# First expert's rows by one-hot products and a hand-written tail: two layers of hybrid attention with a mixture of experts

## The chip, the cores and the metric

One NeuronCore of one Trainium2 chip runs the whole program. The metric is the time of one execution on the device in microseconds (us), the median of several runs. Engines are named as the profile names them: PE (TensorE, with PEld for its weight loads), DVE (VectorE), ACT (ScalarE), POOL (GpSimd) and SP (SyncE, which issues most transfers). L626 is line 626 of the kernel.

## What is computed

Two layers over 512 tokens of 1,024 columns in f32. Each layer mixes tokens by 16 attention heads, adds the result to the residual, normalises, and sends each token to 2 of 16 experts.

```
for l in range(2):
    mix = hybrid_mixer(x, ...)          # 8 MLA heads and 8 sparse (DSA) heads of 64 columns, then @ w_o
    x = layer_norm(ALPHA * x + mix, ln1_g[l], ln1_b[l])
    ffn = grouped_moe(x, ...)           # router, then top-2 of 16 experts
    x = layer_norm(ALPHA * x + ffn, ln2_g[l], ln2_b[l])

# grouped_moe
aff = sigmoid(xt @ router_w); biased = aff + router_bias
g_sel = argmax over 4 groups of (sum of the 2 best biased of the group's 4)
e_idx = the 2 best experts of that group; wts = aff[e_idx] / sum
act = silu(xt @ w_gate[e]) * (xt @ w_up[e]) * gate
out = sum over e of act @ w_down[e]     # 1024 -> 512 -> 1024
```

## The kernel before

**Precision.** A weight is split on the chip into a high and a low f32r part (a *granule*: 128 x 1024 values; `granule`, L163 casts on ACT, L164 subtracts on DVE or POOL), and a product is made of three matmuls (high x high, low x high, high x low). Transposes and the value products of attention run in plain f32; each such product leaves two records in the trace.

**Attention.** `softmax_T` makes one head's probabilities: scores on PE, minimum on DVE, Exp on ACT, scaling on DVE, then four groups of transposes on PE (L499) which ACT copies to SBUF (L501, `pt[kb]`). `pv` multiplies the values of two heads with these copies (L508): per head four products of 512, 384, 256 and 128 columns. The two heads of a pair have 64 output columns each and write the two halves, partitions 0 to 63 and 64 to 127, of one or of two PSUM tiles. The order of the heads is the string `HEADS` (`m0 m1d0 m2d1 m3d2 d3`); which instruction comes next on an engine is set by the framework's scheduler from priorities (`tc.issue_after` shifts one, a manual dependency adds a wait), unless it stands in a `manual_schedule`.

**From the last projection to the first expert.** `mix` multiplies the mixed heads with `w_o` (L626, 384 matmuls a layer) for four tiles of 128 tokens; tile t + 1 runs two steps (`LAG`) behind tile t. `half` then does, for one half of a tile's columns, the residual (L635, DVE), its statistics (L636), four transposes (L190), ACT's copy and the router's logits (L645, PE). `norm` finishes the tile: mean and variance, rsqrt on POOL (L185), the centred and scaled `x1` (L661, L667; for the last tile ACT L669 and POOL L670), the logits `lg` (L663, L664), and the transfer of `x1` to HBM (`xdr`). `route` selects experts with some twenty small DVE operations (L769 to L798) and gives each token a place in its expert's list of at most CAP rows (L805, L809). `warm` issues products that nobody reads (L200).

**Experts.** `fetch(e)` makes one-hot columns of an expert's list (L893), turns them into row numbers with four small matmuls (`index`, L909, L910), and POOL issues an indirect transfer of the 128 rows (L899). `rows_T` transposes the rows (L190) and splits them into `xh`, `xl`; `gate_up` (L931, L932) and `down` (L953) follow, expert by expert, with the next experts' steps placed between products by the table `between`. Before the first expert the largest count is read into registers (L1041), and all engines branch (L1044) over a body for lists longer than CAP, `overflow`; with these inputs the body doesn't run.

Weights come by SP's queue into a pool of 12 tiles of 128 x 2048 (`bigt`), some three experts ahead. PSUM has the pools "mm" (4 tiles), "tr" (2) and "pv" (2).

## Time and profile before

| | |
|---|---|
| median of 3 runs | 1271.31 us (1266.88 to 1273.93) |
| the profiled execution | 1272.13 us, span 1270.3 us |
| busy: PE / DVE / ACT / POOL | 1196.8 / 1040.6 / 805.5 / 313.5 us |
| mean granted clock of PE | 0.968 |
| layer 0: first attention products to the last projection | 140 to 238.4 us |
| layer 0: end of the last projection to the first expert product | 283.25 to 316.04 us |
| layer 0: experts at full pace | 319 to 550 us |

The span runs from the first to the last instruction. Busy times are sums over the span, so an engine with a low share can still be the one that others wait for within a stage; the stages have to be read apart.

### The profile page before, as it was taken

To read this page: it belongs to the slowest core of one execution; us is meant where nothing else is said; L and a number is where in the kernel's file an instruction comes from. 1 tells how busy PE (TensorE), PEld (TensorE's weight loads), DVE (VectorE), ACT (ScalarE), POOL (GpSimd) and SP (SyncE) were. 2 spreads that over 40 slices of the span, in tenths; PEclk is the share of its full clock that TensorE was granted. 3 is DMA by queue.
4 is the path that set the end of the run, shared out by engine and by line. 5 is a ranking of instruction groups with operands and counts; after the bars stand their busy time and mean duration, and the time that the engine had idled before them with its cause. 6 is when DMAs were issued, how large, how long until landed. Compare 5 with 4: busy or idle time off the path is not lost. (4 is left out here: it accounts for less than half of the span.)

```text
span 1270.3 us, 17037 instructions
## 1 busy us (share of the span) xinstructions
PE 1196.8 (94%) x5821; PEld 926.8 (73%) x5821; DVE 1040.6 (82%) x1855; ACT 805.5 (63%) x1262; POOL 313.5 (25%) x241
## 2 busy tenths in 40 slices
PE   9999999996999999999898999999969999999995
PEld 6777555785888888887687775557858888888873
DVE  4689956387999999998858899563779999999897
ACT  4523567532888888887535245665328888888883
POOL 2334323113111111110542343322231111112005
PEclk9989999998999999999898899999989999999998
DMA  7616103374899999987335160033758999999941
GB/s 269 192 45 195 53 1 132 133 265 146 326 390 372 384 385 381 377 323 298 99 128 161 34 231 2 32 115 125 260 192 319 385 385 394 381 376 373 328 169 67
DMA packets 57264, 292.91 MB, mean 231 GB/s; under 512 B 10194, under 2 KB 14034, under 8 KB 28752
## 3 DMA queue, kind: packets, MB, share of 16 engines
q1 hardware_dynamic: 47376, 270.48, 58.3%
q0 software_dynamic: 8352, 16.00, 3.5%
q10 hardware_dynamic: 1440, 5.24, 1.0%
q8 instruction: 49, 0.80, 0.2%
q14 instruction: 47, 0.39, 0.1%
HBM read 269.01 MB, written 31.98 MB: 237 GB/s over the span
## 5 line engine op out<-in xcount | busy, mean ns | idle before, releaser
L163 ACT CAST hl<-big 128x1024 fp32r<-128x1024 f32 x446 | 465.0, 1054 | 147.5 <-PE mm L932 56.5
L164 DVE TENSOR_TENSOR hl<-big,hl 128x1024 fp32r<-128x1024 f32 x407 | 490.0, 1230 | 58.5 <-ACT hl L163 51.3
L931 PE MATMUL mm<-hl,xh 128*128 128x512 f32 x512 | 211.4, 413 | 0.9 <-ACT xh L163 0.9
L932 PE MATMUL mm<-hl,xh 128*128 128x512 f32 x512 | 201.2, 393 | 0.0
L953 PE MATMUL pv<-hl,hT 128*128 128x512 f32 x720 | 169.8, 390 | 2.9 <-DVE big L963 2.9
L953 PEld LDWEIGHTS pv<-hl,hT 128*128 128x128 f32 x720 | 134.8, 188 | 31.8 <-DVE big L963 3.6
L271 PE MATMUL mm<-big,hl 128*128 128x512 f32 (+1 forms) x624 | 147.5, 397 | 1.9 <-ACT big L163 1.1
L271 PEld LDWEIGHTS mm<-big,hl 128*128 128x128 f32 x624 | 118.4, 203 | 27.2 <-ACT hl L163 2.5
L164 POOL TENSOR_TENSOR hl<-big,hl 128x1024 fp32r<-128x1024 f32 x39 | 94.4, 2423 | 159.5 <-ACT hl L163 151.2
L899 POOL DMA_INDIRECT xg<-xdr,ii x32 | 52.7, 1647 | 275.4 <-DVE ii L910 274.8
L931 PEld LDWEIGHTS mm<-hl,xh 128*128 128x128 f32 x512 | 97.1, 190 | 17.3 <-ACT xh L163 1.1
L932 PEld LDWEIGHTS mm<-hl,xh 128*128 128x128 f32 x512 | 97.4, 190 | 16.2
L932 PE MATMUL mm<-hl,xl 128*128 128x512 f32 x256 | 100.7, 394 | 0.0
L931 PE MATMUL mm<-hl,xl 128*128 128x512 f32 x256 | 100.6, 393 | 0.0
L626 PE MATMUL mm<-hl,big 128*128 128x512 f32 x384 | 96.1, 398 | 0.0
L626 PEld LDWEIGHTS mm<-hl,big 128*128 128x128 f32 x384 | 70.3, 188 | 13.1
L501 ACT COPY big<-tr 128x512 f32<-128x512 f32 (+3 forms) x128 | 49.6, 430 | 46.1 <-PE tr L499 45.5
L489 ACT ACTIVATE P<-P,mn 128x128 f32<-128x128 f32 (+3 forms) x128 | 71.4, 562 | 10.8 <-DVE mn L487 10.3
L565 POOL TENSOR_TENSOR mh<-dd,cn 128x256 f32<-128x256 f32 (+2 forms) x64 | 45.9, 739 | 79.5 <-DVE mn L487 40.0
L973 POOL DMA_INDIRECT ydr<-y,ii x26 | 26.4, 1014 | 147.2 <-ACT y L969 123.5
L499 PE MATMUL tr<-cn,P 128*128 128x128 f32 x320 | 58.9, 287 | 3.6 <-DVE P L495 2.9
L499 PEld LDWEIGHTS tr<-cn,P 128*128 128x128 f32 x320 | 37.1, 141 | 33.9 <-ACT big L501 15.8
(259 smaller groups left out, 1883.9 us busy)
## 6 DMA issues: line engine op xcount, KB each, us to landing
big<-wgu SPq DMA_DIRECT2D x128, 1024.0 KB, 7.5
big<-wdn SPq DMA_DIRECT2D x64, 1024.0 KB, 6.9
big<-win SPq DMA_DIRECT2D x10, 1024.0 KB, 5.8
ydr<-zz SPq DMA_DIRECT2D x2, 4096.0 KB
big<-wo SPq DMA_DIRECT2D x8, 1024.0 KB, 14.9
big<-ydr SPq DMA_DIRECT2D x8, 1024.0 KB, 5.0
big<-wqk SPq DMA_DIRECT2D x4, 1024.0 KB, 4.9
big<-dq SPq DMA_DIRECT2D x32, 128.0 KB, 2.3
```

The costliest lines, as they stand in the source:

```text
L163: i = nc.scalar.copy(hi, src).ins
L164: (eng or nc.vector).tensor_sub(lo, src, hi.bitcast(F32))
L271: nc.tensor.matmul(p[:, ts], w[j == 1][:, k * 128:(k + 1) * 128], x, start=(j + k == 0), stop=(j == end and k == 7))
L489: nc.scalar.activation(e, e, AF.Exp, bias=mn[:, i:i + 1], scale=-1.0, accum_out=su[:, i:i + 1])
L499: nc.tensor.transpose(p[:, (i - kb) * 128:(i - kb + 1) * 128], P[:, PO[i] + kb * 128:PO[i] + (kb + 1) * 128], ident)
L501: nc.scalar.copy(pt[kb], p[:, :512 - 128 * kb])
L565: last_mask[0] = nc.gpsimd.tensor_tensor(m[:, c:c + w], dd, C("slope", h, h + 1).to_broadcast([128, w]), op=OP.mult)
L626: R["pe"] = nc.tensor.matmul(pp[t][i], x, w[:, i * 512:(i + 1) * 512], start=first, stop=last).ins
L899: return nc.gpsimd.indirect_dma_start(out=xg, out_offset=None, in_=xdr[l], in_offset=bass.IndirectOffsetOnAxis(ap=ii[:, 0:1], axis=0), bou ...
L931: nc.tensor.matmul(pg, x, w[:, :512], start=(k == 0 and x is a and w is wh), stop=last)
L932: nc.tensor.matmul(pu, x, w[:, 512:], start=(k == 0 and x is a and w is wh), stop=last)
L953: nc.tensor.matmul(py[i], x, w[:, i * 512:(i + 1) * 512], start=(k == 0 and x is a and w is wh), stop=last)
```

## The change

1. In `pv` the first head's product `kb` gets a dependency on the second head's copy `kb`, so that the two heads' products can only be issued when both are ready.
2. `half` and `norm` are cut into `residual`, `turn`, `logits`, `moments` or `squares` (tile 2's variance by an ACT Square with a sum), `inverse`, `centre`, `scores` and `scaled`. For tiles 2 and 3 these stand in an order written by hand for DVE, ACT and PE.
3. GpSimd no longer adds the bias of `x1` or splits granules of the first expert; `first_hi` and `first_lo` split its first four granules on ACT and DVE, two of them before the hand-written stretch.
4. The first expert's rows are no longer fetched and transposed. `places` makes f32 one-hot matrices, and `gather` multiplies the `x1` tiles with them into two PSUM tiles (32 products of 128 columns a layer), from which `rows_T` splits directly.
5. The overflow count is taken in `route_count`, ahead of the rest of the routing, which moves into the first expert's products; a small Silu on ACT stands in the routing.
6. `fetch(1)`'s transfer, `fetch(2)`, `fetch(3)` and the second expert's rows move to later places; all four loads of the third expert's gate and up weights stand after the branch (two stood before it).
7. The overflow body loops over its four tiles, so it has about a quarter of the instructions. `warm` issues 12 products a layer in place of 86.

```diff
-            return pt
+                copies.append(nc.scalar.copy(pt[kb], p[:, :512 - 128 * kb]).ins)
+            return pt, copies
...
-                for p, pt, val, s, _ in heads:
-                    nc.tensor.matmul(p[s * 64:(s + 1) * 64, kb * 128:], val(kb), pt[kb],
-                                     start=(kb == 0), stop=(kb == NT - 1), skip_group_check=True)
+                for n, (p, (pt, _), val, s, _) in enumerate(heads):
+                    i = nc.tensor.matmul(p[s * 64:(s + 1) * 64, kb * 128:], val(kb), pt[kb],
+                                         start=(kb == 0), stop=(kb == NT - 1), skip_group_check=True).ins
+                    if n == 0:
+                        tc.add_manual_dep(i, heads[1][1][1][kb].name,
+                                          mybir.DependencyInfo(mybir.DependencyClass.Sync,
+                                                               mybir.DependencyReason.DATA), reason="with its pair")
...
+        def residual(t, i, stats=True):
 
             if i == 0:
-                xts[t], pls[t], sums[t] = u4p("xt"), ps("pv"), sm.tile([128, 2, 6], F32, name="lns")
+                sums[t] = sm.tile([128, 2, 6], F32, name="lns")
             zi = zs[t][:, i * 512:(i + 1) * 512]
-            nc.vector.scalar_tensor_tensor(zi, zi, ALPHA, pp[t][i], op0=OP.mult, op1=OP.add)
-            nc.vector.bn_stats(sums[t][:, i], zi)
-            end = t == NT - 1 and i == 1
-            if end:
...
+            nc.vector.scalar_tensor_tensor(zi, zi, ALPHA, pp[t][i], op0=OP.mult, op1=OP.add,
+                                           accum_out=None if stats else sums[t][:, i, 0:1])
+            if stats:
+                nc.vector.bn_stats(sums[t][:, i], zi)
+
+        def turn(t, i):
+            if i == 0:
+                xts[t] = u4p("xt")
+            nc.scalar.copy(xts[t][i], transpose4(zs[t], 512 * i))
...
+            if i == 0:
+                pls[t] = ps("pv")
             for k in range(4 * i, 4 * i + 4):
                 R["pe"] = nc.tensor.matmul(pls[t][:, :NE], xts[t][i][:, (k % 4) * 128:(k % 4 + 1) * 128],
                                            wgb[:, k, 0, :], start=(k == 0), stop=(k == 7)).ins
...
+        def squares(t):
+
+            m = mvs[t] = sm.tile([128, 2], F32, name="lnm")
+            nc.vector.tensor_scalar(m[:, 0:1], sums[t][:, 0, 0:1], sums[t][:, 1, 0:1], 1.0 / D, op0=OP.add, op1=OP.mult)
+            pre["x1"].append(x4("x1"))
+            nc.scalar.activation(pre["x1"][t], zs[t], AF.Square, bias=m[:, 0:1], scale=-1.0, accum_out=m[:, 1:2])
...
-                else:
-                    nc.scalar.activation(x1, x1, AF.Copy, scale=rs)
-                    R["x1"] = nc.gpsimd.tensor_add(x1, x1, b).ins
-            (nc.sync if t == NT - 1 else nc.scalar).dma_start(xdr[l][t * 128:(t + 1) * 128, :], x1)
...
+        def places(t):
+
+            if t == 0:
+                pre["oh"] = h2("oh0")
...
+        def gather(t, i):
+
+            for k in range(4):
+                nc.tensor.matmul(pre["xT"][i][:, k * 128:(k + 1) * 128],
+                                 pre["x1"][t][:, i * 512 + k * 128:i * 512 + (k + 1) * 128],
+                                 pre["oh"][:, t * 128:(t + 1) * 128], start=(t == 0 and k == 0),
+                                 stop=(t == NT - 1 and k == 3), skip_group_check=True)
+
+        pre["g0"] = []
+
+        def first_hi(k):
+            t = bigt(F32R).rearrange("p (a b) -> p a b", a=2) if k < 2 else hlp.tile([128, 2, 1024], F32R, name="hl")
+            nc.scalar.copy(t[:, 0], pre["gu", 0][k // 2][:, k % 2 * 1024:(k % 2 + 1) * 1024])
+            pre["g0"].append((t[:, 0], t[:, 1]))
+
+        def first_lo(k):
+            hi, lo = pre["g0"][k]
+            nc.vector.tensor_sub(lo, pre["gu", 0][k // 2][:, k % 2 * 1024:(k % 2 + 1) * 1024], hi.bitcast(F32))
...
+        E = mybir.EngineType
+        for k in range(2):
+            first_hi(k)
+            first_lo(k)
         pre["wd", 0] = load_wd(l, 0)
-        pre["gu", 2] = [load_gu(l, 2, j) for j in range(2)]
-        R["warm"] = ps("mm")
-        for i in range(2):
+        with tc.manual_schedule(engines={E.DVE, E.Activation, E.PE}):
+            residual(2, 0, False)
+            residual(2, 1, False)
+            squares(2)
             for k in range(8 - LAG, 8):
-                mix(3, k, (i,))
-            half(3, i)
-        norm(3)
-        route(R, lg, 2, 4)
+                mix(3, k, (0,))
+            turn(2, 0)
+            turn(2, 1)
+            pre["xT"] = ps("mm"), ps("mm")
+            residual(3, 0)
+            inverse(2, 1.0 / D)
+            centre(2, 0, 1)
+            for k in range(8 - LAG, 8):
+                mix(3, k, (1,))
+            residual(3, 1)
+            moments(3)
+            centre(2, 1, 2)
+            logits(2, 0)
+            logits(2, 1)
+            turn(3, 0)
+            R["warm"] = ps("tr")
+            turn(3, 1)
+            logits(3, 0)
+            gather(0, 0)
+            logits(3, 1)
+            scores(2)
+            centre(3, 0, 1)
+            scores(3)
+            first_hi(2)
+            centre(3, 1, 2)
+            gather(0, 1)
+            gather(1, 0)
+            gather(1, 1)
+            warm(6, R["warm"], R["pe"])
+
+            def while_placing():
+
+                nc.scalar.activation(sm.tile([128, 1], F32, name="lnv"), mvs[2][:, 0:1], AF.Silu)
+                scaled(2, 0, 1)
+
+            route(R, lg, 2, 4, while_placing)
+            first_hi(3)
+            places(2)
+            places(3)
+            cm = route_count(R)
+            scaled(2, 1, 2)
+            scaled(3, 0, 1)
+            scaled(3, 1, 2)
+            gather(2, 0)
+            gather(2, 1)
+            cm()
+            gather(3, 0)
+            gather(3, 1)
+            pre["lo"] = first_lo
...
+        while_placing()
         nc.vector.tensor_mul(R["pos"][:, cs], pc[:, :W], sel)
...
+    def route_count(R):
+
+        cm = sm.tile([128, 2], F32, name="cs")
+        nc.vector.reduce_max(cm[:, 0:1], R["pos"], axis=AX.X)
+
+        def over_tokens():
+            pm = ps("tr")
+            nc.tensor.transpose(pm[0:1, 0:128], cm[:, 0:1], ident)
+            nc.vector.reduce_max(cm[0:1, 1:2], pm[0:1, 0:128], axis=AX.X)
+            R["counted"] = nc.vector.tensor_copy(R["cmi"][0:1], cm[0:1, 1:2]).ins
+
+        return over_tokens
...
-        nc.vector.reduce_max(cmx, R["pos"], axis=AX.X)
-        pm = ps("tr")
-        warm(4, R["warm"], nc.tensor.transpose(pm[0:1, 0:128], cmx, ident).ins)
-        cm1 = scr[:, 4 * W + NT + 1:4 * W + NT + 2]
-        nc.vector.reduce_max(cm1[0:1], pm[0:1, 0:128], axis=AX.X)
-        nc.vector.tensor_copy(R["cmi"][0:1], cm1[0:1])
...
-            p = transpose4(st[e]["xg"], 512 * i)
+            p = transpose4(st[e]["xg"], 512 * i) if e else pre["xT"][i]
             st[e]["c"] = split(xh[:, i * 512:(i + 1) * 512], xl[:, i * 512:(i + 1) * 512], p)
...
-                        stack.enter_context(tc.issue_after((r["rs", 2], r["x1"])[k] if k < 2 else st[1]["i"]))
-                    wh, wl = granule(pre["gu", e][k // 2], k % 2, nc.gpsimd if e == 0 and k < 2 else nc.vector)
+                        stack.enter_context(tc.issue_after(st[0]["c"]))
+                    wh, wl = (pre["g0"][k] if e == 0 and k < len(pre["g0"]) else
+                              granule(pre["gu", e][k // 2], k % 2, nc.vector))
...
-        g0 = fetch(0)
         fetch(1)
-        warm(3, r["warm"], st[1]["pe"])
-        with tc.issue_after(st[1]["i"]):
-            route_rest(r)
-        index(0, 1, 2)
-        index(1, 1, 2)
-        warm(8, r["warm"], st[1]["pe"])
+        with tc.issue_after(r["counted"]):
+            pre["lo"](2)
+            pre["lo"](3)
         with tc.manual_schedule(engines={mybir.EngineType.SP}):
             overflow(l, r)
-            pre["gu", 2] += [load_gu(l, 2, j) for j in (2, 3)]
...
             if e + 1 < NE:
-                between[5] = lambda: rows_T(e + 1, 0)
-                between[6] = lambda: rows_T(e + 1, 1)
+                between[5 if e else 6] = lambda: rows_T(e + 1, 0)
+                between[6 if e else 7] = lambda: rows_T(e + 1, 1)
             if LATE - 1 <= e < NE - 1:
                 between[3] = lambda: late_rows(e + 1)
             if e == 0:
-                between[0] = lambda: fetch(2)
-            if e + 3 < NE:
...
+            if e == 1:
+                between[4] = lambda: fetch(3)
+            if e and e + 3 < NE:
...
-                oe = sm.tile([128, NT], F32, name="o_oe", bufs=1)
-                nc.sync.dma_start(oe, od[bass.ds(e, 1)].rearrange("o p m -> p (o m)"))
-                oi = sm.tile([128, NT], I32, name="o_oi", bufs=1)
-                nc.vector.tensor_copy(oi, oe)
-                for t in range(NT):
+                oe = sm.tile([128, 1], F32, name="o_oe", bufs=1)
+                with tc.For_i(0, NT, 1) as t:
+                    nc.sync.dma_start(oe, od[bass.ds(e, 1), :, bass.ds(t, 1)].rearrange("o p m -> p (o m)"))
+                    oi = sm.tile([128, 1], I32, name="o_oi", bufs=1)
+                    nc.vector.tensor_copy(oi, oe)
                     xr = u4("xr")
```

On PE in layer 0's attention, at the first pair of a latent head (`pv<-big`, values in `vs`) and a sparse head (`pv<-big,oh`). Before:

```order
L508 MATMUL pv<-big 64x384
L508 MATMUL pv<-big 64x256
L508 MATMUL pv<-big 64x128
...
L499 MATMUL tr<-cn,P 128x128 x3
L508 MATMUL pv<-big,oh 64x512
L508 MATMUL pv<-big,oh 64x384
L221 MATMUL mm<-big,hl 128x512
L223 MATMUL mm<-big,hl 128x512 x2
L508 MATMUL pv<-big,oh 64x256
L508 MATMUL pv<-big,oh 64x128
```

and now:

```order
L509 MATMUL pv<-big 64x512
L500 MATMUL tr<-cn,P 128x128
L509 MATMUL pv<-big,oh 64x512
L509 MATMUL pv<-big 64x384
L509 MATMUL pv<-big,oh 64x384
L509 MATMUL pv<-big 64x256
L509 MATMUL pv<-big,oh 64x256
L509 MATMUL pv<-big 64x128
L509 MATMUL pv<-big,oh 64x128
```

The two heads' products stood in two groups, with scores and other work between; now they alternate, and one transpose stands between the first and the second. All 8 pairs of a layer alternate so, in 5 of them with that transpose.

On PE at the end of the last projection (`mm<-hl,big` are its products, `pv<-wgb,xt` the logits, `tr<-cn,z` the transposes of the residual). Before:

```order
L626 MATMUL mm<-hl,big 128x512 x27
L190 MATMUL tr<-cn,z 128x128 x4
L626 MATMUL mm<-hl,big 128x512
L190 MATMUL tr<-cn,z 128x128 x4
L645 MATMUL pv<-wgb,xt 128x16 x4
L626 MATMUL mm<-hl,big 128x512 x3
L645 MATMUL pv<-wgb,xt 128x16 x4
L626 MATMUL mm<-hl,big 128x512 x3
L190 MATMUL tr<-cn,z 128x128 x4
L626 MATMUL mm<-hl,big 128x512 x2
```

and now, with the row products of `gather` (`mm<-oh,x`, here with the numbers of their buffers):

```order
L631 MATMUL mm<-hl,big 128x512 x25
L190 MATMUL tr<-cn,z 128x128 x8
L631 MATMUL mm<-hl,big 128x512 x6
L655 MATMUL pv<-wgb,xt 128x16 x8
L190 MATMUL tr<-cn,z 128x128 x8
L655 MATMUL pv<-wgb,xt 128x16 x4
L720 MATMUL mm<-oh_2311,x_2207 128x128 x4
L655 MATMUL pv<-wgb,xt 128x16 x4
L720 MATMUL mm<-oh_2311,x_2207 128x128 x4
L720 MATMUL mm<-oh_2311,x_2270 128x128 x8
```

The last products of tile 3 now stand ahead of all logits of tiles 2 and 3, and the first row products between the logits.

On POOL from the tail's last operations to the branch. Before:

```order
L164 TENSOR_TENSOR hl<-big,hl 128x1024
L185 TENSOR_TENSOR lny<-lnv,mhalf 128x1
L670 TENSOR_TENSOR x_2547<-x_2547,lnp 128x1024
L164 TENSOR_TENSOR hl<-big,hl 128x1024
L899 DMA xg<-xdr_83,ii 128x1024 x2
L1041 TENSOR_LOAD r_cmi
L1044 COMPARE_AND_BRANCH
```

and now (the rows between the branch and its end are the body that is jumped over):

```order
L164 TENSOR_TENSOR hl<-big,hl 128x1024
L185 TENSOR_TENSOR lny<-lnv,mhalf 128x1 x2
L1170 TENSOR_LOAD r_cmi
L1173 COMPARE_AND_BRANCH
...
L1173 UNCONDITIONAL_BRANCH
L1023 DMA xg<-xdr_83,ii 128x1024 x4
```

The bias add and a granule are gone, the first expert's transfer is gone, and the second expert's stands behind the branch.

## Rows read from the trace of the kernel before

**Rows 1.** The page, parts 1 and 5: busy time; line, operation, mean ns, idle.

```profile
PE 1196.8 (94%) x5821; PEld 926.8 (73%) x5821; DVE 1040.6 (82%) x1855; ACT 805.5 (63%) x1262; POOL 313.5 (25%) x241
...
L164 DVE TENSOR_TENSOR hl<-big,hl 128x1024 fp32r<-128x1024 f32 x407 | 490.0, 1230 | 58.5 <-ACT hl L163 51.3
```

**Rows 2.** Windows: length, busy of PE, PEld, DVE, ACT, POOL, clock, DMA share, GB/s.

```profile
140.00:160.00 20.00, 18.56 (x79) 10.80 (x78) 18.48 (x54) 11.07 (x31) 9.47 (x13) 1.00 0.01 2
160.00:238.40 78.40, 76.75 (x359) 44.90 (x358) 44.83 (x157) 50.22 (x155) 20.34 (x29) 1.00 0.23 81
...
283.20:316.00 32.80, 22.53 (x184) 18.36 (x182) 25.74 (x66) 7.39 (x12) 12.19 (x7) 0.89 0.37 122
316.00:319.00 3.00, 2.96 (x7) 2.34 (x8) 2.67 (x11) 0.47 (x1) 0.98 (x1) 0.50 0.97 358
319.00:550.00 231.00, 231.00 (x1141) 189.58 (x1141) 218.75 (x262) 198.38 (x231) 37.84 (x28) 1.00 0.98 372
```

**Rows 3.** Timeline, layer 1's tail: start, duration, engine, line, operation, count, wait before.

```profile
914.73 1.29 DVE L635 SCALAR_TENSOR_TENSOR z<-z,mm 128x512 f32<-128x512 f32 x2 [3.66 <-PE mm L626]
...
947.55 0.80 PE L931 MATMUL mm<-hl,xh 128*128 128x512 f32 x1
```

**Rows 4.** Windows of line L508 alone, both layers: length, PE, PEld, clock, DMA.

```profile
120.00:240.00 120.00, 37.21 (x128) 13.67 (x128) 1.00 0.26 92
750.00:875.00 125.00, 37.21 (x128) 13.67 (x128) 1.00 0.29 104
```

**Rows 5.** Timeline of PE in layer 0's attention.

```profile
137.99 2.37 PE L508 MATMUL pv<-big 128*64 128x512 f32 x14
...
173.06 2.37 PE L508 MATMUL pv<-big,oh 128*64 128x512 f32 x8
...
205.92 1.07 PE L508 MATMUL pv<-big 128*64 128x512 f32 x2
```

**Rows 6.** Timeline of DVE in layer 0's tail.

```profile
283.25 1.28 DVE L635 SCALAR_TENSOR_TENSOR z<-z,mm 128x512 f32<-128x512 f32 x2 [3.66 <-PE mm L626]
...
292.82 0.67 DVE L635 SCALAR_TENSOR_TENSOR z<-z,mm 128x512 f32<-128x512 f32 x1
...
296.32 0.23 DVE L664 SCALAR_TENSOR_TENSOR lg<-lg,lny,c 128x16 f32<-128x16 f32 x1
297.58 2.32 DVE L769 SCALAR_TENSOR_TENSOR route<-r_gm,rbt 128x32 f32<-128x32 f32 x1 [1.03 <-ACT r_gm L768]
299.93 2.25 DVE L773 TENSOR_TENSOR route<-route 128x24 f32<-128x24 f32 x1
...
304.08 0.19 DVE L798 SCALAR_TENSOR_TENSOR r_sel<-route 128x32 bf16<-128x32 f32 x1
...
308.50 0.13 DVE L838 CAST r_cmi<-route 1x1 int32<-1x1 f32 x1
```

**Rows 7.** Timeline of PE in layer 0's tail.

```profile
277.70 6.42 PE L626 MATMUL mm<-hl,big 128*128 128x512 f32 x27
...
287.03 0.96 PE L645 MATMUL pv<-wgb,xt 128*128 128x16 f32 x8
...
314.04 1.06 PE L190 MATMUL tr<-cn,xg 128*128 128x128 f32 x8 [2.79 <-PEq L1044]
...
316.04 0.79 PE L931 MATMUL mm<-hl,xh 128*128 128x512 f32 x1 [0.86 <-ACT xh L163]
```

**Rows 8.** Timeline of POOL in layer 0's tail.

```profile
297.50 2.34 POOL L670 TENSOR_TENSOR x<-x,lnp 128x1024 f32<-128x1024 f32 x1 [1.26 <-ACT x L669]
299.80 2.34 POOL L164 TENSOR_TENSOR hl<-big,hl 128x1024 fp32r<-128x1024 f32 x1
```

**Rows 9.** Waits: SP, 300 to 320 us; ACT, 319 to 560: us, times, longest.

```profile
SPq L1044 <- SPq L1044: 4.2, 1, 4.2
...
ACT hl L163 <- DMA big<-wgu: 0.9, 3, 0.3
```

**Rows 10.** One line's page, L899: from issue to landing.

```profile
DMA to landing us min/median/max: 5.0/6.9/10.1
```

More of the change, by code (lines that the diff above doesn't have):

```diff
@@ L174, in granule @@
             eng = nc.gpsimd if nlo[0] % POOL_EVERY == 0 else nc.vector
-        t = hlp.tile([128, 2, 1024], F32R, name="hl")
+        t = hlp.tile([128, 2, 1024], F32R, name="hl") if tile is None else tile
         split(t[:, 0], t[:, 1], raw[:, g * 1024:(g + 1) * 1024], eng)
@@ new lines, in half, with moments @@
+        def half(t, i):
+            residual(t, i)
+            turn(t, i)
+            logits(t, i)
+        mvs, rss = {}, {}
+        def moments(t):
+            mvs[t] = sm.tile([128, 2], F32, name="lnm")
+            nc.vector.bn_aggr(mvs[t], sums[t].rearrange("p a b -> p (a b)"))
+            return inverse(t, 1.0)
+        def squares(t):
[3 more added lines that the diff above has]
+            nc.scalar.activation(pre["x1"][t], zs[t], AF.Square, bias=m[:, 0:1], scale=-1.0, accum_out=m[:, 1:2])
```

119 lines of the change are left out of this document (67 added, 52 removed).

## The prediction

> **What bounds the kernel now.** I read the profile from the whole to the part: first the busy shares, then tables by stage, then the timelines of the two stages that the change touches. PE is busy 94% of the span [rows 1], so a gain must come from PE work that disappears or from the few stretches in which PE waits. The table by stage [rows 2] shows both. From 160 to 238.4 us (attention of layer 0) PE works 76.75 of 78.40 us, at full clock, with DVE at 57% and ACT at 64%: there the number of PE passes sets the time. From 140 to 160 us DVE works 18.48 of 20 us, as much as PE. From 283.2 to 316 us (end of the last projection, routing, first rows) PE is busy 22.53 of 32.80 us and DVE 25.74, and part of PE's work there is filler (the L200 products), so a chain through several engines sets the time. From 319 to 550 us PE works all of 231.00 us and the DMA engines 98%: fewer instructions elsewhere buy nothing there. Layer 1 repeats it: its tail, from the same DVE instruction to the first expert product, takes 947.55 − 914.73 = 32.82 us [rows 3]. Every term below is per layer and counts twice.
>
> **Attention: value products in pairs.** The 128 records of L508 (64 products, each left in two records) keep PE busy 37.21 us in each layer [rows 4]. One head's four products in one run take 2.37 us, at 173.06 [rows 5]. At 137.99 seven products, of two heads and so of different 64-column halves, also take 2.37 us: standing next to each other they ran at the same time and the narrower half was free. A first product of 512 columns that stands alone takes 1.07 us, at 205.92 [rows 5]. In the new order all 8 pairs stand together; in 5 of them one transpose separates the first product from the rest. That makes 8 × 2.37 + 5 × 1.07 = 24.3 us, 12.9 us less than 37.21.
>
> The Trainium skill, "TensorE: Matmul & The Clock Gate", section "Measured speedup vs the span model", speaks against a free second half: three column tiles gave 2.38 times, not 3. At that efficiency a pair would cost about 2.98 us (an estimate by that page), 4.9 us less of gain. The row with seven products in 2.37 us contradicts it here, so the sum goes by the row.
>
> Not all of 12.9 us will be seen. The first product of a pair now also waits for the second head's copies, and everything behind it on PE (scores and transposes of the next heads) waits with it, so DVE and ACT get their next input later. The trace has no such wait. Lower bound: each of the 8 pairs loses about one lone product, 8 × 1.07, which leaves 4.3 us; upper bound 12.9. The pair that lies in 140–160, where DVE is the bound, gives nothing; in the rest DVE and ACT would still be under 80% busy when the time shrinks by a tenth. I take 9 us, a little above the middle.
>
> **Tail, in five pieces.** T is 283.25, the start of DVE's residual of tile 2 [rows 6]. The first product of the first expert starts at 316.04 [rows 7].
>
> (a) T to the residual of tile 3's second half: 292.82 − 283.25 = 9.57 us. The last products of tile 3 stand between transposes, logits and the norm of tile 2. New order: both halves of tile 2's residual (1.28 us), the last four transposes (half of the 1.06 us that eight take, 0.53), six products at 6.42 / 27 = 0.24 us each [rows 7]. That is 1.28 + 0.53 + 1.43 = 3.2; I take 3.4.
>
> (b) From there to the logits on DVE: 296.32 + 0.23 − 292.82 = 3.73 us. This piece grows: what was done before (a) now lies in it. PE has eight transposes (1.06), sixteen logit products (four groups of 0.96 us, by the row at 287.03) and four row products, f32 with 128 columns, which I price as one more such group: 1.06 + 5 × 0.96 = 5.9, and some 0.5 for the last two operations on DVE: 6.4 us.
>
> (c) Logits to the selection, 296.55 to 304.27 = 7.72 us. L769 took 2.32 us and L773 2.25 us, though L773 has only 24 columns; they end within 0.06 us of the two GpSimd operations beside them, L670 and L164 of 2.34 us each [rows 6, 8]. All else up to 304.27 took 2.09 us after L773. Both GpSimd operations are removed. With 0.2 us for each of the two: 1.03 (the wait for ACT's r_gm) + 0.4 + 2.09 = 3.5; 4.0 because the order of ACT's work changes. Where the adds go: they become DVE passes of 0.6 to 1.3 us, put behind the selection while PE computes positions, and before the branch.
>
> (d) Selection to the cast of the count, 304.27 to 308.63 = 4.36 us. The count is taken earlier but two one-hot operations stand before it: 4.4 us, unchanged.
>
> (e) Cast to first product, 308.63 to 316.04 = 7.41 us. In it lie SP's 4.2 us at the branch [rows 9] and PE's 2.79 us for its own sequencer at L1044, then eight transposes (1.06) [rows 7] and an ACT table load beside them. The transposes and the table load go off this path, as does the transfer of the first rows. The body that the branch jumps over shrinks to a quarter. If the wait at the branch goes with it, DVE's two lo granules (1.23 us each [rows 1], ahead of its branch) and the split of the rows set the pace: 2 × 1.23 + 0.94 (from the end of the transposes to the first product, now for the split) + some 0.9 for reading the count = 4.3 us. If it stays: 5.41 (308.63 to 314.04) + 0.94 = 6.4 us.
>
> Sum: 3.4 + 6.4 + 4.0 + 4.4 + (4.3 to 6.4) = 22.5 to 24.6 in place of 32.8, so 8.2 to 10.3 us saved; I take 9. Bounds: 6, if (a) and (b) together save nothing but the GpSimd holds and transposes go (4.2 + 2); 12, if the last row products are also hidden behind DVE.
>
> **Edits costed at nothing.** The second expert's indirect transfer now stands behind the branch on POOL. It lands after 5.0 to 10.1 us [rows 10] and is needed 36 products, about 8.5 us at 0.24 each, after the first expert begins; without that cover PE waits up to 2 us. All four loads of the third expert's gate and up weights come after the branch on SP's queue (two before): two tiles more of 128 × 2048 × 4 bytes, 2.1 MB, 5.6 us at 372 GB/s [rows 2]. Three experts' weights are ahead, and ACT waited only 0.9 us in three waits for such a load in the whole stretch [rows 9]. The 74 filler products per layer that go cost nothing, if the row products keep PE's clock: after its 2.79 us wait PE had 0.50 of the clock, the 1.2 GHz level, from 316 to 319 [rows 2], which costs 1.5 us now and may stay.
>
> **Sum.** 2 × (9 + 9) = 36 us. The profiled execution took 1272.13 us, 0.8 above the median of three: 1272.13 − 36 = 1236.
>
> **The rivals.**
>
> R1, the pairs save no time: DVE and ACT bind where PE no longer does. For: DVE at 92% in 140–160, ACT at 64% in 160–238 [rows 2]; a paired result needs both heads' copies early. Against: most of the stage has 35% slack. If 2 us of the 12.9 remain: 2 × (2 + 9) = 22, 1250 us. The Trainium skill, "TensorEngine Tiling (Array Packing)", section "PSUM Bottleneck", names this course: tiling speeds TensorE but not the copies out of PSUM. No run here shows yet which it is.
>
> R2, the start of the experts stays slow: the branch wait remains (6.4 and not the middle 5.4: −1.0), the second expert's rows land late (−2), and PE still starts at 0.50 (−1.5). The tail then saves 4.5: 2 × (9 + 4.5) = 27, 1245 us. For: the order on POOL, and the routing stretch with little filler. Against: landings at the median of 6.9 are in time.
>
> R3, slower: the pair's wait holds PE for most of a head. Sixteen heads take 98.4 us (140 to 238.4), 6.15 each; if PE stands for 5 us at each pair, 16 × 5 = 80 against 42 gained: 1310 us. It decides from 2 × (12.9 + 9) / 16 = 2.7 us per pair on. For: PE's queue is in order and the first product waits. Against: PE's own order puts the second head's transposes ahead of it, so the wait is one copy, not a head.
>
> R4, weights late after the branch: 2 × 5.6 = 11 more, 1247 us. Against: the 0.9 us.
>
> R5, both upper bounds: 2 × (12.9 + 12) = 50, 1222 us.
>
> **How the numbers follow.** Forecast 0.58, its own range 1226 to 1246 (2 × 5 us either way); R1 0.15, R2 0.13, R4 0.03, R5 0.05, R3 0.03; and 0.03 for R1 and R2 together (2 × (2 + 4.5) = 13, 1259 us). Range 1222 to 1253: it leaves out R3, the case of R1 with R2, and the edges of R1 and R5. A difference of 0.5% (6.4 us) is about what a measurement of this kernel can tell from none. Faster: all but R3 and the worst of the joint case, 0.94; same 0.025; slower 0.035.
>
> **What would show it.** Right: L509 busy near 24 us per layer in place of 37.21, attention shorter by about 9; no DVE operation of 24 columns above 0.3 us in the routing; the residual of tile 3 within 4 us of tile 2's; no transposes of xg before the first expert; SP's wait at the branch under 2 us; PE fully busy in the experts' stage as before. Wrong: PE waits for ACT's copies ahead of the pairs above 1 us each (R1, R3); ACT waiting for weights (R4); PE waiting for the second expert's rows, or 0.50 of the clock beyond 3 us (R2).

## The result and the profile after

The changed kernel takes 1239.07 us (median of 4 runs, 1236.97 to 1243.3) against 1270.28 for the kernel before in the same comparison: a ratio of 0.9758, with a 95% interval of 0.972 to 0.9796. The forecast was 1236 in a range of 1222 to 1253. The profiled execution took 1238.69 us.

From its page, the span and part 1 (busy time, share, number of instructions):

```profile
span 1236.9 us, 16946 instructions
...
PE 1168.2 (94%) x5777; PEld 918.9 (74%) x5777; DVE 1033.9 (84%) x1875; ACT 803.8 (65%) x1264; POOL 292.6 (24%) x233
```

PE's busy share is 94% as before [rows 1]; its busy time fell by 28.6 us, nearly as much as the span (33.4). That the two agree proves nothing: the value products fell by 25.8 us, but the filler products (L200), which cost no time, also fell, from 29.7 to 7.0 us, and the row products came in. What was won has to be read by stage.

The value products, same view as [rows 4]:

```profile
120.00:240.00 120.00, 24.32 (x128) 10.95 (x128) 0.97 0.29 105
730.00:860.00 130.00, 24.32 (x128) 10.95 (x128) 1.00 0.31 112
```

24.32 us in place of 37.21 in each layer; the forecast had 24.3. (The granted clock of 0.97 in layer 0 comes back below.) A whole pair on PE's timeline, to be read against the lone head of [rows 5]:

```profile
171.98 0.64 PE L509 MATMUL pv<-big 128*64 128x512 f32 x1
171.99 0.64 PE L509 MATMUL pv<-big,oh 128*64 128x512 f32 x1
...
174.08 0.27 PE L509 MATMUL pv<-big 128*64 128x128 f32 x1
174.09 0.27 PE L509 MATMUL pv<-big,oh 128*64 128x128 f32 x1
```

The second head's record starts 0.01 us behind the first's, and both end together: 16 records in 174.36 − 171.98 = 2.38 us, the time of one head before.

The tail on DVE, answering [rows 6]:

```profile
274.64 0.69 DVE L640 SCALAR_TENSOR_TENSOR z<-z,mm 128x512 f32<-128x512 f32 x1 [0.95 <-PE mm L631]
...
278.50 0.69 DVE L640 SCALAR_TENSOR_TENSOR z<-z,mm 128x512 f32<-128x512 f32 x1
...
284.54 0.24 DVE L694 SCALAR_TENSOR_TENSOR lg<-lg,lny,c 128x16 f32<-128x16 f32 x1
...
285.35 0.19 DVE L883 SCALAR_TENSOR_TENSOR route<-r_gm,rbt 128x32 f32<-128x32 f32 x1
285.57 0.18 DVE L887 TENSOR_TENSOR route<-route 128x24 f32<-128x24 f32 x1
...
288.45 0.19 DVE L912 SCALAR_TENSOR_TENSOR r_sel<-route 128x32 bf16<-128x32 f32 x1
...
292.44 0.13 DVE L934 CAST r_cmi<-cs 1x1 int32<-1x1 f32 x1
```

and on PE, answering [rows 7]:

```profile
295.77 0.50 PE L1059 MATMUL mm<-big,xh 128*128 128x512 f32 x1 [1.92 <-ACT xh L163]
...
319.24 0.63 PE L190 MATMUL tr<-cn,xg 128*128 128x128 f32 x4 [1.05 <-DMA xg<-xdr,ii]
```

T is 274.64 now (283.25 before), and the first product comes 21.1 us later (32.8 before). The two small routing operations that took 2.32 and 2.25 us take 0.19 and 0.18. The second row on PE is a new wait: the rows of the third expert come 1.05 us too late.

By the same two marks in every kernel's timeline, and two more, the time can be laid out by layer. "Start" is T in layer 0, and in layer 1 T less the start of layer 0's last `down` record; "tail" is from T to the first expert's first product; "first expert" goes on to the first `down` product (it holds the gate and up products of the first two experts); "last experts" is from the 18th of the 12th expert's 24 `down` products to the start of the last one. Each cell has layer 0 / layer 1, in us of the profiled execution; what is between does not differ by more than 0.2.

| kernel | median | start | tail | first expert | last experts |
|---|---|---|---|---|---|
| before | 1268.8 to 1271.3 | 283.25 / 305.98 | 32.8 / 32.8 | 26.1 / 26.1 | 64.2 / 64.4 |
| after | 1239.1 | 274.64 / 295.31 | 21.1 / 22.7 | 28.7 / 27.8 | 66.4 / 66.3 |
| pair_only | 1250.5 | 275.05 / 294.19 | 31.8 / 33.0 | 26.3 / 25.0 | 64.1 / 64.4 |
| no_pair | 1257.7 | 283.29 / 304.69 | 21.1 / 25.2 | 28.8 / 28.6 | 64.9 / 65.2 |
| no_pool_adds | 1260.6 | 283.52 / 303.76 | 28.3 / 28.0 | 26.3 / 26.3 | 64.1 / 64.2 |
| small_body | 1265.9 | 283.34 / 305.69 | 29.5 / 32.1 | 25.1 / 26.4 | 64.1 / 64.2 |
| three_edits | 1239.4 | 275.61 / 295.25 | 26.1 / 27.3 | 25.0 / 26.6 | 64.2 / 64.3 |
| padded_body | 1242.9 | 273.76 / 294.90 | 24.0 / 26.0 | 27.4 / 28.3 | 66.5 / 66.4 |
| last_order | 1239.0 | 274.36 / 295.23 | 25.3 / 25.2 | 26.7 / 28.1 | 64.2 / 64.8 |
| pair_all | 1230.0 | 268.54 / 290.70 | 21.1 / 22.6 | 28.5 / 28.0 | 64.8 / 65.3 |
| warm_branch | 1238.4 | 273.71 / 294.93 | 21.2 / 22.7 | 27.5 / 28.1 | 66.3 / 66.4 |
| best | 1231.7 | 269.81 / 291.64 | 24.6 / 25.8 | 28.1 / 27.0 | 64.3 / 64.7 |
| three_all | 1232.4 | 270.44 / 291.41 | 25.5 / 27.5 | 25.4 / 26.2 | 64.1 / 64.3 |
| best2 | 1225.2 | 269.92 / 289.71 | 23.7 / 25.2 | 27.3 / 26.9 | 64.3 / 64.7 |

After against before: 8.6 and 10.7 us won in front of the tail, 11.7 and 10.1 in it, and then 2.6 and 1.7 given back in the first expert and 2.2 and 1.9 in the last ones. That is 41.1 less 8.4, or 32.7 of the 33.4 us of span. The starts are one execution each and vary: `before`, `no_pair`, `no_pool_adds` and `small_body` have the same attention without pairs, and layer 1's start is between 303.76 and 305.98 us in them.

The stretch of the last experts, windows with the columns of [rows 2], after and then before:

```profile
544.87:567.15 22.28, 20.22 (x103) 16.55 (x101) 18.13 (x19) 16.01 (x20) 0.98 (x1) 1.00 0.72 252
567.15:585.80 18.65, 18.65 (x79) 15.26 (x77) 16.31 (x16) 15.29 (x16) 0.00 (x0) 0.91 0.90 337
```

```profile
562.52:584.20 21.68, 20.23 (x103) 16.55 (x102) 17.93 (x19) 16.01 (x20) 0.99 (x1) 1.00 0.67 239
584.20:601.25 17.05, 17.05 (x78) 14.09 (x77) 15.49 (x17) 14.82 (x16) 0.00 (x0) 1.00 0.97 364
```

PE waits 0.6 us more in the first stretch, and the second, fully busy, has a granted clock of 0.91: part of it ran at 0.50, the 1.2 GHz level, and it is 1.6 us longer. The wait in question, 1.46 us before, is now:

```profile
566.81 0.50 PE L1081 MATMUL pv<-hl,hT 128*128 128x512 f32 x1 [2.06 <-DVE big L1091]
```

### The profile page after: what moved, and what is told of

Read it like the earlier page. It is cut to its first block, busy times and chain, and to the rows that moved or that the text cites. A ratio compares the mean times of both kernels' runs of the same rounds, so it can differ in the third digit from the quotient of the medians.

```text
span 1236.9 us, 16946 instructions
## 1 busy us (share of the span) xinstructions
PE 1168.2 (94%) x5777; PEld 918.9 (74%) x5777; DVE 1033.9 (84%) x1875; ACT 803.8 (65%) x1264; POOL 292.6 (24%) x233
## 4 chain that ended last, share of the span: by engine, by line
PE 56%; DVE 10%; issue 4%; POOL 2%; DMA 2%; ACT 2%; POOLq 0%; DVEq 0%; ACTq 0%
PE pv L1081 14%; PE mm L1059 13%; PE mm L1060 13%; PE tr L190 4%; PE mm L631 3%; PE mm L271 2%; PE pv L509 2%; PE tr L500 2%; DVE aw L366 1%; DMA xg<-xdr,ii 1%; POOL x L1214 1%; DVE m L365 1%; PE mm L543 1%; DVE aw L358 1%; PE pv L655 1%
## 5 line engine op out<-in xcount | busy, mean ns | idle before, releaser
L163 ACT CAST hl<-big 128x1024 fp32r<-128x1024 f32 x438 | 457.6, 1054 | 132.5 <-PE mm L1060 62.7
L1059 PE MATMUL mm<-hl,xh 128*128 128x512 f32 x504 | 207.1, 411 | 0.0
L1060 PE MATMUL mm<-hl,xh 128*128 128x512 f32 x504 | 197.3, 391 | 0.0
L1081 PE MATMUL pv<-hl,hT 128*128 128x512 f32 x720 | 173.0, 395 | 4.1 <-DVE big L1091 4.1
L1081 PEld LDWEIGHTS pv<-hl,hT 128*128 128x128 f32 x720 | 137.2, 191 | 33.9 <-DVE big L1091 4.8
L271 PEld LDWEIGHTS mm<-big,hl 128*128 128x128 f32 x624 | 116.1, 199 | 28.3 <-ACT hl L163 3.9
L164 POOL TENSOR_TENSOR hl<-big,hl 128x1024 fp32r<-128x1024 f32 x35 | 85.4, 2443 | 162.7 <-ACT hl L163 154.4
L1060 PEld LDWEIGHTS mm<-hl,xh 128*128 128x128 f32 x504 | 95.2, 189 | 15.8
L1059 PEld LDWEIGHTS mm<-hl,xh 128*128 128x128 f32 x504 | 95.0, 188 | 15.5
L1060 PE MATMUL mm<-hl,xl 128*128 128x512 f32 x252 | 98.7, 392 | 0.0
L1059 PE MATMUL mm<-hl,xl 128*128 128x512 f32 x252 | 98.5, 391 | 0.0
L500 PEld LDWEIGHTS tr<-cn,P 128*128 128x128 f32 x320 | 36.4, 141 | 38.8 <-ACT big L502 21.2
L570 POOL TENSOR_TENSOR mh<-dd,cn 128x256 f32<-128x256 f32 (+2 forms) x64 | 43.5, 701 | 77.1 <-DVE q L528 21.1
## 6 DMA issues: line engine op xcount, KB each, us to landing
ydr<-zz SPq DMA_DIRECT2D x2, 4096.0 KB, 13.4
```

Source lines behind the costliest of these rows:

```text
L163: i = nc.scalar.copy(hi, src).ins
L164: (eng or nc.vector).tensor_sub(lo, src, hi.bitcast(F32))
L271: nc.tensor.matmul(p[:, ts], w[j == 1][:, k * 128:(k + 1) * 128], x, start=(j + k == 0), stop=(j == end and k == 7))
L500: nc.tensor.transpose(p[:, (i - kb) * 128:(i - kb + 1) * 128], P[:, PO[i] + kb * 128:PO[i] + (kb + 1) * 128], ident)
L1059: nc.tensor.matmul(pg, x, w[:, :512], start=(k == 0 and x is a and w is wh), stop=last)
L1060: nc.tensor.matmul(pu, x, w[:, 512:], start=(k == 0 and x is a and w is wh), stop=last)
```

## The experiments

Theory A, from the table: the two parts of the change add up; the pairs give about 19 us, the tail about 22, of which some 8 are given back further on. Each run has its own rival.

**The pairs alone, and the rest alone.** `pair_only` puts the new `pv` into the kernel before; `no_pair` takes it out of the changed one:

```diff
-                    if n == 0:
-                        tc.add_manual_dep(i, heads[1][1][1][kb].name, ...)
```

> The kernel before with the paired value products alone. Theory A (the two parts of the change add up): the pairs give what the traces show in front of the tail, 8.6 us in layer 0 and 10.7 in layer 1, so about 1270 - 19 = 1251 us, the tail stays at 32.8 us in each layer, and the last expert loses nothing. Rival B (the gain ahead of the tail comes from elsewhere, or is given back where DVE and ACT are late): 1258 us or more.

> The changed kernel without the dependency that makes pairs. Theory A: the tail of 21 to 23 us stays, the 19 us of the pairs are lost: about 1239 + 19 = 1258 us, with the records of the value products back at 37 us a layer. Rival B: under 1250 us.

Measured: 1250.51 us (ratio 0.9849, 0.9821 to 0.9877) and 1257.73 us (0.99, 0.9877 to 0.9924). The pairs are worth 20.6 us alone and 18.7 on top of the rest; the rest 13.4. The sum, 34, is what the two have together within 3 us. Rival B is out. The last experts lose 0.8 us a layer in `no_pair`, nothing in `pair_only`, and 2.0 in the changed kernel.

**GpSimd operations moved to DVE** in the kernel before, three passes a layer (the last tile's bias add and two granules):

```diff
-                    R["x1"] = nc.gpsimd.tensor_add(x1, x1, b).ins
+                    R["x1"] = nc.vector.tensor_add(x1, x1, b).ins
-                    wh, wl = granule(pre["gu", e][k // 2], k % 2, nc.gpsimd if e == 0 and k < 2 else nc.vector)
+                    wh, wl = granule(pre["gu", e][k // 2], k % 2, nc.vector)
```

> The kernel before with the two GpSimd operations of the tail (bias add of the last tile, two granules of the first expert) put on DVE, nothing else. Theory A (GpSimd held DVE): the operations of 32 and 24 columns in the routing fall from 2.3 us to under 0.3; DVE pays 1.2 us for each moved pass; 1 to 3.7 us a layer are left, 1263 to 1268 us. Rival C (DVE, in order, does the moved passes in the same place, so nothing is won): within 2 us of 1270.

Measured: 1260.63 us (0.9922, 0.9898 to 0.9947), 10.5 us less, more than either theory said. Its tail on DVE:

```profile
295.11 0.24 DVE L664 SCALAR_TENSOR_TENSOR lg<-lg,lny,c 128x16 f32<-128x16 f32 x1
295.83 1.22 DVE L670 TENSOR_TENSOR x<-x,lnp 128x1024 f32<-128x1024 f32 x1 [0.49 <-ACT x L669]
296.98 0.18 DVE L769 SCALAR_TENSOR_TENSOR route<-r_gm,rbt 128x32 f32<-128x32 f32 x1
297.08 1.22 DVE L164 TENSOR_TENSOR hl<-big,hl 128x1024 fp32r<-128x1024 f32 x1
298.22 0.17 DVE L773 TENSOR_TENSOR route<-route 128x24 f32<-128x24 f32 x1
```

Two passes of 1.22 us now stand in the chain, yet logits to selection takes 5.1 us in place of 7.7, since L769 and L773 fall from 2.3 us to under 0.2. Rival C is out. What I had not reckoned with is ahead of it: the other moved granule, of 2.37 us on GpSimd at 289.30, had held DVE too. The second operation of tile 2's logits, 128 by 16 values, took 2.10 us beside it and takes 0.22 now:

```profile
289.60 2.10 DVE L664 SCALAR_TENSOR_TENSOR lg<-lg,lny,c 128x16 f32<-128x16 f32 x1
```

```profile
289.85 0.22 DVE L664 SCALAR_TENSOR_TENSOR lg<-lg,lny,c 128x16 f32<-128x16 f32 x1
```

So the residual of tile 3's second half starts 7.66 us after T, not 9.57.

**The loop in the overflow body**, alone in the kernel before (`small_body`), and its reverse, 120 more PE instructions in the body of the changed kernel (`padded_body`):

```diff
+            for _ in range(15):
+                transpose4(scr, 0)
+                transpose4(scr, 512)
             with tc.For_i(0, NE, 1) as e:
```

> The kernel before with the looped overflow body alone. Theory A (the branch over a long body holds PE): PE's branch instruction falls from 3.7 and 4.7 us to about 0.3, as in the changed kernel; the first expert's rows then bind, which land about 312 to 314 us in layer 0, so 0.3 to 2.1 us a layer are won, 1266 to 1269 us. Rival D (the length of the body doesn't matter): the branch stays at 3.7 us, no change.

> The changed kernel with 120 more PE instructions (transposes, never executed) in the overflow body, so that PE jumps as far as before. Theory A: PE's branch instruction takes 3.7 us or more again, PE reaches the first expert 2 us late in layer 0 and about 1 in layer 1: 1239 + 3 = 1242 us. Rival D (the number of instructions doesn't matter, the short wait comes from when the engines arrive): branch 0.3 us, 1239 us.

Measured: 1265.94 us (0.9969, 0.9955 to 0.9983), 5.2 us less; and 1242.88 us (0.9773, 0.9756 to 0.9789), 3.8 us more than the changed kernel, though the two intervals overlap, so that here the traces decide. PE's branch instruction (count, shortest / median / longest in ns, starts) before, after, in `small_body` and in `padded_body`:

```profile
L1044 PEldq COMPARE_BRANCH  x2: 3748/4240/4732, 309.9 to 941.2; - x2
```

```profile
L1173 PEldq COMPARE_BRANCH  x2: 318/335/352, 294.0 to 907.4; - x2
```

```profile
L1044 PEldq COMPARE_BRANCH  x2: 219/288/358, 309.0 to 936.6; - x2
```

```profile
L1173 PEldq COMPARE_BRANCH  x2: 3792/3820/3848, 293.1 to 910.5; - x2
```

On PE the length of the body decides between 0.3 and 3.7 to 4.7 us; instructions that never run cost it, and rival D is out. In `padded_body` PE's wait ahead of the first product is 4.8 us in layer 0 (1.9 in the changed kernel), and from the cast of the count to that product it takes 2.9 us more in layer 0 and 0.8 in layer 1; the rest of layer 1's longer tail is a stretch at half clock in the logits. SP has a stall of the same kind, not in the branch itself but ahead of its next instruction. SP's waits before in layer 1 (layer 0's 4.2 us is in [rows 9]), then after in layers 0 and 1:

```profile
SPq L1044 <- SPq L1044: 3.6, 1, 3.6
```

```profile
SPq L1173 <- SPq L1173: 1.3, 1, 1.3
...
SPq L1173 <- SPq L1173: 3.0, 1, 3.0
```

So 4.2 and 3.6 us became 1.3 and 3.0: in layer 1 SP stalls over the short body too, and since ACT goes on only when SP has let it, the first product waits there. In layer 0 of the changed kernel ACT's row is:

```profile
295.13 1.07 ACT L163 CAST xh<-mm 128x512 fp32r<-128x512 f32 x2 [7.65 <-SPq L1173]
```

`small_body` is the same: no wait of SP in layer 0, 3.7 us in layer 1, and its tail is 3.3 us shorter in layer 0 and 0.7 in layer 1. That the body's length makes SP's stall is therefore not shown: over the same short body it took nothing in one layer and as much as before in the other. Where neither engine stalls any more, PE has a next wait (layer 0 of `small_body`):

```profile
311.53 1.06 PE L190 MATMUL tr<-cn,xg 128*128 128x128 f32 x8 [0.89 <-DMA xg<-xdr,ii]
```

The first expert's rows arrive at 311.5 us, 2.5 us before the point (314.04, [rows 7]) at which PE had been let go.

**Three edits without hand order and row products.** The pairs, the two moved GpSimd operations and the looped body, in the kernel before.

> The kernel before with three of the change's edits: the pairs, the GpSimd operations of the tail on DVE, the looped overflow body. No hand order, no row products, the first expert's rows still come by transfer. The runs so far gave 20.6, 10.5 and 5.2 us for them one by one. Theory A (the pieces add up, and the hand order with row products buys little beyond them): about 1271 - 36 = 1235 us, not slower than the changed kernel's 1239. Rival E (the body and the GpSimd operations shorten the same path, which then waits for the first expert's rows, so that only the row products get the rest): 1240 us or more.

Measured: 1239.4 us (0.9744, 0.9728 to 0.976), the time of the changed kernel. Its tail is longer (26.1 and 27.3 against 21.1 and 22.7 us), but the first expert (25.0 and 26.6) and the last ones (64.2) give nothing back. It also waits for the first expert's rows, 1.04 us in layer 0, which is rival E's mechanism; the sum is 4 us short of what the pieces gave singly, so the time lies between the two theories. No run has the hand order without the row products or the reverse, so what each of the two is worth is not known.

**The order of the last experts.** On ACT and DVE the changed kernel splits the 15th expert's hidden rows before it empties the first half of the 14th's output; the kernel before had them the other way round. A dependency puts that back (`i` is the split's copy or subtraction, `j` the output's):

```diff
+            if e == NE - 2:
+                for i, j in zip(ii, first_part):
+                    tc.add_manual_dep(i, j.name, ...)
```

> The changed kernel with the order of before at one place of the last experts: on ACT and DVE the first half of the first joined output stands ahead of the split of the next expert's hidden rows. Theory A (this swap delays PE by 0.6 us, PE's wait then is 2.1 us, and the granted clock falls behind it): the stretch of the last experts goes back from 66.3 to 64.2 us in both layers, 1239 - 4 = 1235 us, with no stretch below full clock there. Rival F (the clock falls there for another reason, such as the work before): 0.6 us a layer, 1238 us.

Measured: the stretch goes back to 64.2 and 64.8 us, with PE's wait at 1.5 us and a granted clock of 1.00 in the windows that had 0.91. So the swap is what the stretch loses by, as theory A has it. That the wait by itself brings the clock down is not so: `no_pair` and `pair_all` have the swap and the same wait, in both layers, and full clock behind it. `no_pair`'s row, and the window behind it:

```profile
575.73 0.50 PE L1077 MATMUL pv<-hl,hT 128*128 128x512 f32 x1 [2.06 <-DVE big L1087]
```

```profile
576.00:594.30 18.30, 18.30 (x84) 15.12 (x84) 16.49 (x17) 15.76 (x18) 0.00 (x0) 1.00 0.93 342
```

In the kernels with the wait of 2.06 us (two layers each) the clock fell in the changed kernel, `padded_body` and `warm_branch`, and did not in these two; behind 1.46 us, in all the others, it never fell. So the swap costs 0.6 to 0.9 us a layer where the clock holds and 1.9 to 2.3 where it falls, and of rival F it stays open what else has to come to the wait.

The kernel takes 1239.02 us (0.9742, 0.9726 to 0.9758), no less than the changed one. In the profiled execution the tails took it back, 25.3 and 25.2 us, not 21.1 and 22.7; the other executions have no trace. Windows of layer 0's tail, `last_order` and then the changed kernel:

```profile
274.36:299.63 25.27, 22.52 (x149) 21.17 (x147) 18.07 (x55) 7.51 (x13) 1.93 (x3) 0.80 0.36 126
```

```profile
274.64:295.77 21.13, 17.78 (x149) 16.51 (x148) 17.99 (x55) 7.50 (x13) 1.94 (x3) 1.00 0.42 151
```

The same 149 PE records and the same DVE work, but 4.7 us more on PE at a clock of 0.80. PE's timeline of `last_order` there, two rows that take 1.14 and 0.96 us in the changed kernel:

```profile
282.45 2.05 PE L720 MATMUL mm<-oh,x 128*128 128x128 f32 x8
284.30 1.73 PE L655 MATMUL pv<-wgb,xt 128*128 128x16 f32 x8
```

So the hand-written tail has two lengths, some 3 to 4 us apart, by whether PE runs logits and row products at 2.4 or at 1.2 GHz. The profiled executions of the changed kernel, `pair_all` and `warm_branch` and layer 0 of `no_pair` and `padded_body` had the short one, those of `last_order`, `best` and `best2` and layer 1 of `no_pair` and `padded_body` the long one. PE's waits in the 12 us ahead are the same in the changed kernel and `last_order`, 0.3 and 0.2 us, so no wait of PE tells them apart, and what decides it stays open.

**Pairs that wait for the second copy**, so that no transpose can stand inside a pair:

```diff
-                        tc.add_manual_dep(i, heads[1][1][1][kb].name, ...)
+                        tc.add_manual_dep(i, heads[1][1][1][max(kb, 1)].name, ...)
```

> The changed kernel with the pair's first product waiting for the second head's second copy, so that all 16 products of a pair stand together and the lone product of 1.0 us in 5 of 8 pairs is gone. If two heads really run at the same time and PE is the bound: up to 5 us a layer less, about 3 after the longer wait, 1233 us, and 18.4 us for the products of a layer. Rival G (DVE and ACT bind in the stage): no change in time, though the records fall to 18.4 us.

Measured: 1229.97 us (0.9694, 0.9655 to 0.9732; runs from 1225.8 to 1237.5). The value products take 20.06 us a layer, 4.3 less than in the changed kernel, with one pair of eight still cut in two:

```profile
120.00:240.00 120.00, 20.06 (x128) 8.75 (x128) 1.00 0.28 104
```

Start is 6.1 us shorter in layer 0 and 4.6 in layer 1. The interval just touches the changed kernel's (0.972 to 0.9796), but the same edit in `three_all` below gives 7.0 us again. Rival G is out; the forecast 18.4 us was not reached, because of that one pair.

**Products after the branch.** Twelve unread products between the branch and the first expert:

```diff
             pre["gu", 2] = load_gu(l, 2)
+        warm(6, ps("tr"), r["counted"])
```

> The changed kernel with 12 products that nobody reads behind the branch, ahead of the first expert's first product, in the 1.9 and 3.5 us in which PE waits there. If the half clock behind that wait (3.4 us of it in layer 0) comes from the wait: PE runs the first expert at full clock, 1.5 us a layer less, 1236 us. Rival I (the clock there depends on the whole stretch ahead): 0.5 of the clock stays at the start of the first expert, 1239 us.

Measured: 1238.36 us (0.9768, 0.9742 to 0.9795), no difference. In layer 0 they filled PE's wait but for 0.66 us, the first expert's start had full clock, and it took 27.5 us, 1.2 less. In layer 1 PE still waited 1.8 us behind them, and had 0.50 of the clock again. So where the wait went, the half clock went; the kernel's time does not show it. But the wait is not the whole cause here either: layer 0 of `last_order` has a wait of 1.90 us ahead of the first product and a granted clock of 1.00 behind it, after a tail with 0.50 in it. So rival I is not out.

**Four fixes together.** `best` has `pair_all`, `last_order`, the third expert's rows fetched at the first expert's third step, and the two low granules ahead of the count; `best2` leaves the granules where the change has them. `three_all` is `three_edits` with the longer wait of `pair_all`.

```diff
-                between[7] = both(lambda: fetch(2), between[7])
+                between[2] = lambda: fetch(2)
```

> The changed kernel with four edits: pairs that wait for the second copy (as in pair_all), the order of the last experts (as in last_order), the third expert's rows fetched at the first expert's third step instead of its last, and the two low granules ahead of the count instead of behind it. Theory A: pair_all's 1230 us, less 0.6 to 2 us a layer at the last experts, 0.4 to 1.0 for the third expert's rows, about 1 for the granules: 1225 us. Rival H (granules ahead of the count stand in the routing chain and cost what they save, and PE at half clock in the tail swamps the rest): 1230 us, no difference.

> The kernel before with the three edits of three_edits and pairs that wait for the second copy, and nothing else of the change. Theory A (the pieces add up): 1239.4 - 9 = 1230 us, level with pair_all, which has the hand order and the row products too. Rival E (hand order and row products are worth something of their own): 5 us or more above pair_all in the same call's terms, 1235 us.

> The kernel of best with the low granules back behind the count, as the change has them. Theory A (the granules in the routing chain cost what they saved): about 2 us a layer less than best in the routing, 1227 us. Rival J (where PE's half clock falls in the tail decides between these kernels): 1230 to 1232 us as best and pair_all, with the tail at 25 us where PE has 0.50 of its clock in it and 21 where not.

Measured: `best` 1231.69 us (0.9692, 0.967 to 0.9714), `three_all` 1232.4 us (0.9708, 0.9689 to 0.9728), `best2` 1225.15 us (0.9642, 0.9617 to 0.9667). `best` is as slow as rival H said, `best2` as fast as its theory A or a little faster, so rival J's 1230 us is out: in `best` logits to selection took 4.9 us against 3.9 in `best2`, as a granule of 1.2 us stood in the chain. The profiled executions differ by 4.1 us: 1.4 in the two tails, 0.9 in the first experts, and 1.9 in layer 1's start, where `best` had 3.4 us more at 0.50 of the clock; both had half clock in their tails. No wait for the third expert's rows is left in `best2`, and its first expert takes 27.3 and 26.9 us. `best2` is the fastest kernel here, 45 us under the kernel before and 14 under the changed one. `three_all` lies 2.4 us above `pair_all`, nearer theory A than rival E, but its interval is wholly above that of `best2`: with the order of the last experts and the late fetch put right, the rest of the change (hand order, row products, other fetch order) is worth some 7 us on top of the three edits.

## Why the prediction was right, step by step

**Pairs.** 9 us a layer forecast, 8.6 and 10.7 seen; the busy time to the digit. The 12.9 us of PE work did not all turn into time. PE now waits 5.3 us in layer 0's attention (3.6 before): 2.0 for DVE's minima, 1.4 for its scaled rows, 1.4 for a latent copy. And in layer 0 the 0.97 above is a stretch at 0.50 of the clock, from 154.5 to 161.4 us: from the first value product to T this execution takes 137.2 us, against 135.8 for the same code without that stretch in `padded_body` and `warm_branch`. So 1.4 of the 4.3 us that are missing there belong to the clock. R1 fell: 4 of 12.9 us went, not 11. So did R3: no wait ahead of a pair reached 1 us, where it would have needed 2.7. The lone products were not a given but a cost, as `pair_all` shows: about 5 us a layer lay in them.

**Tail.** Forecast and measured in layer 0, by the five pieces:

| piece | before | forecast | measured |
|---|---|---|---|
| (a) to the last residual | 9.57 | 3.4 | 3.86 |
| (b) to the logits | 3.73 | 6.4 | 6.28 |
| (c) to the selection | 7.72 | 4.0 | 3.86 |
| (d) to the cast of the count | 4.36 | 4.4 | 3.93 |
| (e) to the first product | 7.41 | 4.3 to 6.4 | 3.20 |

(a) fell for two reasons, and the prediction had one: by `no_pool_adds` 1.9 of its 5.7 us come from the GpSimd granule beside tile 2's logits, the rest from the new order. For (c) the mechanism is shown by `no_pool_adds`. (e) was mis-sized in layer 0, on the good side: two engines stalled, PE in its branch and SP behind it, and both got shorter. In layer 1, where SP still lost 3.0 us, the piece took 4.75 us, inside the range. The term that was wrong is DVE's two granules, 2 × 1.23 us, which were to set the pace once the wait had gone. The first product waits for ACT's copy and not for DVE (the row at 295.77), and ACT for SP (the row at 295.13); in `best`, where the granules stand earlier, the piece still takes 2.9 and 4.2 us.

The Trainium skill, "SBUF — State Buffer", section "Who interferes with whom", says that a DVE instruction with two SBUF inputs contends with a GpSimd instruction that reads SBUF, for a pair of ports that only one of them can hold. The traces agree: 2.25 us for 24 columns beside a GpSimd pass of 2.34 [rows 6, 8], 0.17 without one.

The Trainium skill, "Runtime: NRT & Kernel Launch", section "Instruction fetch mechanics", says that a taken branch to a target outside the instructions at hand stalls for a fetch. PE's 3.7 to 4.7 us against 0.2 to 0.4 agree. SP's stall of 3.0 and 3.7 us in layer 1, over the short body, is not settled by it; why SP keeps it there was not tried.

**What was priced at nothing and was not.** R2 named three delays at the start of the experts. The branch wait went on PE and shrank on SP (to 1.3 us in layer 0; in layer 1 its 3.0 us are above the 2 us named as a sign of being right). The rows that came late, by 1.05 and 0.4 us, were the third expert's, whose fetch I had listed as moved and not costed, not the second's. The 0.50 of the clock stayed, as the prediction allowed: it cost 1.5 us before and 1.7 now (half of 3.0 and of 3.4 us). Together the first expert takes 2.6 and 1.7 us longer, so the clock is little of that: in layer 0 it is 1.4 us of waits (the third expert's rows, and 0.3 for DVE's `xl`), 0.3 for twelve more `index` products, 0.2 of clock, and some 0.7 in the other products, whose cause was not tried. R4 did not come: ACT waited 0.6 us for weights in layer 0's experts.

No step of mine looked at the last experts, 250 us behind the change: there the scheduler turned two instructions round, PE waited 2.1 us instead of 1.5, and in this execution the clock fell behind it. That is 4.1 us for both layers. Pairs and tail gave 41.1 us, 5 more than the 36 forecast, and 8.4 were given back. That the total came within 3 us of the forecast is in part luck: the two errors, a tail mis-sized by some 4 us and losses that were not costed, have opposite signs. (In R3 the 42 us gained should read 43.8, 2 × (12.9 + 9), which changes nothing.)

## What to carry to other kernels

Products of 64 output columns for two heads cost one head's time if nothing, not even one transpose, stands between them in PE's order; wait a little longer for the second head's input. Before a tail is written anew by hand, try its cheap causes singly: here, on top of the pairs, three GpSimd passes a layer moved to DVE and a shorter body behind a branch that skips it came to the same time as the whole change with its hand order, row products and new fetch order. Those paid, by some 7 us, only with two losses that the change had caused elsewhere put right. After any change of order, compare stretches far behind it too, and look at the granted clock there.

## What the runs showed of the hardware that was not expected

PE's branch over a body that doesn't run took 3.5 to 4.7 us where the body holds 144 products (four tiles of 36) and 3.8 where it holds 156, and 0.2 to 0.4 us over 36. SP lost 3.2 to 4.2 us behind its branch over the long body, and between nothing and 3.7 us over the short one. ACT, POOL and DVE took under 0.1 us for their branches over either. A wait of PE of 2.06 us among the last experts was followed by 0.50 of the clock for some 3 us in three kernels and by full clock in two, a wait of 1.46 us at the same place was always followed by full clock. And the same 149 PE records of logits and row products took 17.8 us of PE in some executions and 22.5 in another, the granted clock being 1.00 or 0.80 in that stretch. What decides the clock in these two cases is open.
